# Part of the input projection's weight remainders made ahead, in the first feed-forward, and read back from memory

## The chip, the cores and the metric

One core of a Trainium2 chip runs the whole kernel. The metric is the device time of one execution in microseconds (us), as the median of several runs.

## The reference, cut to what matters

One decoder layer works on 264 tokens (256 of a prompt, 8 of separate samples) of width 2048, all in fp32:

```
h += 1/2 * RMSNorm(SwiGLU_1(RMSNorm(h)))                 2048 -> 2 x 5632 -> 2048
u  = RMSNorm(h);  proj = u @ w_in                        2048 -> 10288 columns: GLU a, b | z | xBC | dt
v  = GLU -> causal depthwise conv (31) -> LayerNorm -> swish
y  = conv (4) on xBC -> SiLU -> chunked state-space scan (48 heads, 8 groups) -> norm gated by SiLU(z)
h += RMSNorm(concat(v, y) @ w_out)                       4096 -> 2048
h += 1/2 * RMSNorm(SwiGLU_2(RMSNorm(h)))
h += RMSNorm(sigmoid(RMSNorm(h) @ W_gate) * (p @ W_proj))
```

Outputs are h and the new convolution and scan states. The change touches only how the weights of `u @ w_in` reach the matrix engine.

## The kernel before, in words

**Three matmuls for one.** Every product with a weight is made in a reduced form of fp32 (`F32R`), with operands split in a high part and a remainder: `x = x_hi + x_lo`, `w = w_hi + w_lo`. `mm3` (L248 to L252) issues `w_hi*x_hi` (L250), `w_hi*x_lo` (L251) and `w_lo*x_hi` (L252) into one accumulator. In the profile `acc` is the accumulator, `act` a split activation (both halves), `whi` and `wlo` the two halves of a weight.

**Weight units.** `PLAN` (L74 to L112) lists all weights in the order of their use as units of at most 16 blocks of 128x128. `Weights.load` (L138 to L157) fetches a unit in two chunks of up to eight blocks (128 partitions x 1024 columns, 512 KB). For each chunk it does three steps: SyncE's queue (SP) issues the DMA `wraw<-in_w` (L153), ScalarE (ACT) rounds it to `whi` (L154), and VectorE (DVE) subtracts `whi` from `wraw` to give `wlo` (L155). Four buffers each of `wraw`, `whi` and `wlo` are two units. `next` (L159) asks for units two ahead of the one in use. A buffer of `whi` or `wlo` comes free when TensorE (PE) has done the last matmul of the chunk four chunks earlier; a buffer of `wraw` comes free when DVE has subtracted the chunk four chunks earlier.

**Stages.** Units 0 to 136 are the first feed-forward (88 gate and up columns, 48 down columns), 137 and 138 the product with `W_proj` (`pproj`), 139 to 219 the 81 units of the input projection, then come the output projection, the second feed-forward and the gate. A unit of 16 blocks is 48 matmuls. `gemm_first` (L340) runs the first units of a matrix with the input index outermost, since its inputs arrive one by one: units 139 to 142 hold four columns (`dt`, B, C, x of group 0) for four of the 16 input blocks each. `gemm_one` (L356) does one column with its 16 input blocks.

**Into the input projection.** L533 to L542 make `u`: for each of 16 blocks k, `tmp = y*rs` (DVE, or GpSimd (POOL) for odd k), `h += tmp` (POOL), two steps later `tmp = h*gain*r` (DVE), a rounding on ACT (L258) and a subtraction on DVE (L259, in the profile L216 `act<-tmp,act`). L545 to L546 then save h in four quarters (`hsave<-h`, on SP's queue).

**Through the input projection.** The loop over `IN_ORDER` (the columns: B, C, three x, three z of each of eight groups, with pairs of GLU columns between) does for each column the convolution or activation on DVE and ACT; after a group's third x column comes `ssd`, whose matmuls, transposes and small DMAs (`ab` L702, `ea` L710, `d_bc` L785, `cbc` L787, `h<-in_hst` L792) run beside the next columns. `finish_gate` closes a group: DVE multiplies y with z (L216 `h<-h,h`, 128x792), ACT squares three parts, POOL adds them (L216 `run<-run,tmp`), PE sums over partitions (L306 `ps<-run,ones`), and ACT and DVE scale. `do_dt` (L571) sends two small arrays through memory (`d_dt`, `d_cs`) before the first `ab` can be loaded.

**Order.** The order of each engine's instructions is set by the framework's scheduler, which places them by a simulated timeline; `load` runs at raised priority. Every engine takes its own list in order, SP's queue of DMAs included: a DMA that waits for a buffer holds all DMAs behind it.

Of the kernel before, what the change touches and what calls it, by code (L numbers as in the profile page):

```python
# [9 lines left out]
F32 = mybir.dt.float32  # L10
F32R = mybir.dt.float32r
AF = mybir.ActivationFunctionType
ALU = mybir.AluOpType
# [6 lines left out]
P = 128  # L20
# [53 lines left out]
def _plan():  # L74

    plan = []
    k16 = list(range(KD))

    def ffn(i):
        gu = f"gu{i}"  # L80
        for q in range(8):
            plan.append((gu, k16[2 * q : 2 * q + 2], list(range(FIRST_FF))))
        for lo, hi in FF_CHUNKS:
            for m in range(max(2 * lo, FIRST_FF), 2 * hi):
                plan.append((gu, k16, [m]))
            for m in range(KD):
                plan.append((f"dn{i}", list(range(lo, hi)), [m]))

    ffn(1)
    for q in range(2):  # L90
        plan.append(("pp", [0, 1], list(range(8 * q, 8 * q + 8))))
    first = [m for _, m in IN_ORDER[:4]]
    for q in range(4):
        plan.append(("in", k16[4 * q : 4 * q + 4], first))
    for _, m in IN_ORDER[4:]:
        plan.append(("in", k16, [m]))
    for q in range(6):
        plan.append(("out", list(range(CM + 4 * q, CM + 4 * q + 4)), [0, 1, 2, 3]))
    for m in range(4, KD, 2):
        for q in range(3):  # L100
            plan.append(("out", list(range(CM + 8 * q, CM + 8 * q + 8)), [m, m + 1]))
    for m in range(0, KD, 2):
        plan.append(("out", list(range(CM)), [m, m + 1]))
    ffn(2)
    for q in range(8):
        plan.append(("pg", k16[2 * q : 2 * q + 2], list(range(FIRST_PG))))
    for m in range(FIRST_PG, KD):
        plan.append(("pg", k16, [m]))
    return plan


PLAN = _plan()  # L112


_COLS = {}
_off = 0
for _n, _w in (
# [10 lines left out]
class Weights:  # L128
# [1 line left out]

    AHEAD = 2

    def __init__(self, tc, pool, w):
        self.tc, self.pool, self.w = tc, pool, w
        self.at = 0
        self.done = []

    def load(self, between=()):  # L138

        tc, nc, i = self.tc, self.tc.nc, len(self.done)  # L140
        n = len(PLAN[i][1]) * len(PLAN[i][2])
        src = self.w[i, :, : n * P].rearrange("p (n c) -> p n c", n=n)
        tiles = []
        with nullcontext() if between else tc.high_priority(offset=1000):
            for a in range(0, n, 8):
                if a // 8 < len(between):
                    between[a // 8]()
                m = min(8, n - a)
                raw, hi, lo = (
                    self.pool.tile([P, 8, P], t, tag=tag, bufs=bufs, name=f"{tag}{i}_{a}")[:, :m, :]  # L150
                    for t, tag, bufs in ((F32, "wraw", 4), (F32R, "whi", 4), (F32R, "wlo", 4))
                )
                self.dma = nc.sync.dma_start(raw, src[:, a : a + m, :])  # L153
                nc.scalar.copy(hi, raw)  # L154
                nc.vector.tensor_tensor(out=lo, in0=raw, in1=hi.bitcast(F32), op=ALU.subtract)  # L155
                tiles += [(hi[:, k, :], lo[:, k, :]) for k in range(m)]
        self.done.append(tiles)  # L157

# [10 lines left out]
def kernel(ctx: ExitStack, tc: tile.TileContext, a: dict):  # L169
    nc = tc.nc  # L170
# [4 lines left out]
    wpool = ctx.enter_context(tc.tile_pool(name="wpool", bufs=4))  # L175
# [4 lines left out]
    dram = ctx.enter_context(tc.tile_pool(name="dram", bufs=1, space=bass.MemoryType.DRAM))  # L180
# [30 lines left out]
    def V(name, i=0):  # L211
        o = _COLS[name][0] + i
        return vec[:, o : o + 1]

    def tt(out, in0, in1, op, eng=None):
        return (eng or nc.vector).tensor_tensor(out=out, in0=in0, in1=in1, op=op)  # L216

    def stt(out, in0, scalar, in1, op0, op1):
        return nc.vector.scalar_tensor_tensor(  # L219
            out=out, in0=in0, scalar=scalar, in1=in1, op0=op0, op1=op1  # L220
        )
# [18 lines left out]
    def act(out, in_, func, bias=0.0, scale=1.0):  # L240
        if func in TABLES:
            table(TABLES[func])
        i = nc.scalar.activation(out=out, in_=in_, func=func, bias=bias, scale=scale)  # L243
        if func in TABLES:
            after(i.ins)
        return i

    def mm3(acc, wt, x, first, last):  # L248
        hi, lo = wt
        nc.tensor.matmul(acc, hi, x[:, 0, :], start=first, stop=False)  # L250
        nc.tensor.matmul(acc, hi, x[:, 1, :], start=False, stop=False)  # L251
        return nc.tensor.matmul(acc, lo, x[:, 0, :], start=False, stop=last).ins  # L252

    def split(x, gain=None):

        t = act_tile()
        if gain is None:
            nc.scalar.copy(t[:, 0, :], x)  # L258
            tt(t[:, 1, :], x, t[:, 0, :].bitcast(F32), ALU.subtract)  # L259
        else:  # L260
            act(t[:, 0, :], x, AF.Identity, scale=gain)
            stt(t[:, 1, :], x, gain, t[:, 0, :].bitcast(F32), ALU.mult, ALU.subtract)
        return t

    class SumSq:
# [3 lines left out]
        def __init__(self, n, tag="run", pool=None, direct=1, fast=False, eng=None, urgent=False):  # L269
            self.n, self.i, self.tag, self.pool = n, 0, tag, pool or apool  # L270
            self.eng, self.urgent = eng or nc.gpsimd, urgent
            self.direct, self.fast, self.parts = direct, fast, []
# [53 lines left out]
    eps1 = cpool.tile([P, 1], F32, name="eps1")  # L326
    nc.gpsimd.memset(eps1, EPS)

    ws = Weights(tc, wpool, a["w"])


    h4 = [h_tile() for _ in range(4)]
# [1 line left out]
    def H(k):  # L334
        return h4[k // 4][:, k % 4, :]
# [18 lines left out]
        return accs  # L354

    def gemm_one(xs, kts, nunits=1):  # L356
        acc = acc_tile()
        n = 0
        for _ in range(nunits):
            for wt in ws.next():  # L360
                mm3(acc, wt, xs[kts[n]], n == 0, n == len(kts) - 1)
                n += 1
        assert n == len(kts)
        return acc

    def ffn(xs, sq, done):
# [27 lines left out]
        def column(m):  # L394
            return accs[m] if m < FIRST_FF else gemm_one(xs, k16)

        ys = [None] * KD
        for c, (lo, hi) in enumerate(FF_CHUNKS):
            for f in range(lo, hi):
                g = gate(column(2 * f))  # L400
                mid(f, g, column(2 * f + 1))
                if bg and f % 2 and f > 2:
                    bg.popleft()()
            for m in range(KD):
                acc = gemm_one(mids, list(range(lo, hi)))
# [50 lines left out]
    ep = ectx.enter_context(tc.tile_pool(name="early", bufs=1))  # L456
# [25 lines left out]

    bg.append(hist_ssm)
    bg.append(hist_mod)


    ysq, hy, yy = (SumSq(KD, f"run{i}", ep, urgent=not i) for i in range(3))
# [32 lines left out]
    for q in range(2):  # L520
        w = ws.next()
# [12 lines left out]
    for k in range(KD + 2):  # L534
        if k < KD:
            t = tmp()
            tt(t, ys[k], rs, ALU.mult, nc.gpsimd if k % 2 and k > 2 else nc.vector)
            tt(H(k), H(k), t, ALU.add, nc.gpsimd if k else nc.vector)
        if k >= 2:
            t = tmp()  # L540
            stt(t, H(k - 2), V("mix_pre", k - 2), r, ALU.mult, ALU.mult)
            us.append(split(t))  # L542
    ectx.close()
    hsave = dram.tile([P, KD, T], F32, name="hsave")
    for q in range(4):  # L545
# [10 lines left out]
        out=tri, in_=tri, pattern=[[1, P]], compare_op=ALU.is_ge, fill=0.0, base=0, channel_multiplier=-1  # L556
# [438 lines left out]
    for k in TAIL_TENSOR:  # L995
        p = tps.tile([P, T], F32, tag="sum", bufs=3, name=nm("sum"))
# [167 lines left out]
```

## Time and profile before

| | |
|---|---|
| median of three runs | 2429.63 us (2427.08 to 2433.99) |
| the profiled execution: its own time, and its span | 2432.44 us, 2430.7 us |
| PE, DVE, ACT, POOL busy, share of the span | 97%, 65%, 49%, 12% |
| DVE's weight subtractions (L155) | 812, 986.9 us in all |
| ACT's weight roundings (L154) | 812, 829.9 us in all |
| moved by DMA, mean rate | 489.89 MB, 202 GB/s |

The span runs from the first to the last instruction of the profiled execution; the 1.7 us between it and the execution's time lie around it. Times in the profile count from the start of the span. The first feed-forward runs to about 772 us, the product with `W_proj` to about 789 us, the input projection to about 1360 us. A row of the windows gives a stretch, its length, the busy time of each engine with its number of instructions, then the clock that TensorE was granted (1.00 is full), the mean busy share of the 16 DMA engines, and GB/s. A row of the waits names who waited for whom, the total in us, how often, and the longest.

### The profile page before, as it was taken

The numbers are of one execution on the slowest core, as the hardware profiler recorded it, in microseconds if no ns is written. First come the engines' busy times: TensorE is split into PE (matmuls) and PEld (weight loads), VectorE is DVE, ScalarE is ACT, GpSimd is POOL, SyncE is SP. The second block draws the span as 40 slices with busy tenths as digits, with TensorE's granted clock in tenths as the row PEclk, the third lists the DMA queues.
The fourth block names the chain that finished last, engine by engine and source line by source line (L and its number), as shares of the span: only waits on it lengthen the run. The fifth ranks groups of instructions, "written<-read, shape, count | busy, mean of one in ns | idle before, by whom it ended". The sixth has DMA issues, their size and how long they took to land.

```text
span 2430.7 us, 47409 instructions
## 1 busy us (share of the span) xinstructions
PE 2367.7 (97%) x19448; PEld 2342.7 (96%) x19448; DVE 1569.2 (65%) x2333; ACT 1181.4 (49%) x1771; POOL 298.4 (12%) x295
## 2 busy tenths in 40 slices
PE   8999999999999889999999999999999999999988
PEld 8999999999999889999999999999999999999988
DVE  6554455545557858988798975766545565565585
ACT  6444444433456465665565545544444443344465
POOL 0400000000015212122122010101000000000103
PEclk9999999999999999999999999999999999999999
DMA  7655555555556666666666556476766776676553
GB/s 249 217 183 184 182 183 182 183 183 183 183 169 207 213 180 193 207 216 202 210 216 205 181 181 216 153 238 228 240 213 223 237 236 217 217 236 206 184 191 132
DMA packets 166250, 489.89 MB, mean 202 GB/s; under 512 B 25568, under 2 KB 42640, under 8 KB 166032
## 3 DMA queue, kind: packets, MB, share of 16 engines
q1 hardware_dynamic: 166032, 486.86, 62.0%
q8 instruction: 152, 2.49, 0.4%
q14 instruction: 66, 0.54, 0.1%
HBM read 465.65 MB, written 22.42 MB: 201 GB/s over the span
## 4 chain that ended last, share of the span: by engine, by line
PE 84%; DVE 6%; issue 3%; ACT 3%; DMA 2%; POOL 1%; SPq 0%; ACTq 0%; POOLq 0%; DVEq 0%
PE acc L250 27%; PE acc L251 27%; PE acc L252 27%; DVE wlo L155 2%; DVE y L219 1%; ACT whi L154 1%; PE ps L306 1%; DVE h L216 1%; DMA ab<-d_cs 1%; DMA cbc<-d_bc 1%; DVE ych L794 1%; PE ps L250 0%; ACT tmp L243 0%; DMA d_bc<-rows 0%; PE ps L251 0%
## 5 line engine op out<-in xcount | busy, mean ns | idle before, releaser
L252 PE MATMUL acc<-act,wlo 128*128 128x264 f32 x6224 | 1770.7, 285 | 4.3 <-DVE wlo L155 4.1
L251 PE MATMUL acc<-act,whi 128*128 128x264 f32 x6224 | 1756.6, 283 | 6.3 <-DVE act L216 6.2
L250 PE MATMUL acc<-act,whi 128*128 128x264 f32 x6224 | 1747.7, 283 | 3.4 <-DVE tmp L216 2.1
L155 DVE TENSOR_TENSOR wlo<-wraw,whi 128x1024 fp32r<-128x1024 f32 (+2 forms) x812 | 986.9, 1217 | 597.9 <-ACT whi L154 595.5
L154 ACT CAST whi<-wraw 128x1024 fp32r<-128x1024 f32 (+2 forms) x812 | 829.9, 1026 | 961.9 <-PE acc L251 717.3
L250 PEld LDWEIGHTS acc<-act,whi 128*128 128x128 f32 x6224 | 1175.5, 190 | 6.0 <-issue 2.1
L251 PEld LDWEIGHTS acc<-act,whi 128*128 128x128 f32 x6224 | 1169.2, 188 | 9.9 <-DVE act L216 7.9
L252 PEld LDWEIGHTS acc<-act,wlo 128*128 128x128 f32 x6224 | 1167.9, 188 | 8.3 <-DVE wlo L155 6.4
L216 POOL TENSOR_TENSOR run<-run,tmp 128x264 f32<-128x264 f32 x93 | 87.8, 944 | 962.9 <-ACT tmp L243 961.8
L216 POOL TENSOR_TENSOR s<-s,eap 128x1024 f32<-128x1024 f32 x24 | 48.8, 2035 | 630.4 <-DMA s<-in_hst 630.4
L219 DVE SCALAR_TENSOR_TENSOR y<-v,vec,y 128x251 f32<-128x251 f32 (+23 forms) x240 | 118.1, 512 | 1.2
L219 DVE SCALAR_TENSOR_TENSOR s<-bb,xds,s 128x128 f32<-128x128 f32 x192 | 52.7, 346 | 66.1 <-POOL s L216 66.1
L216 POOL TENSOR_TENSOR h<-h,cbc 128x512 f32<-128x512 f32 x48 | 73.6, 1553 | 166.0 <-DMA cbc<-d_bc 90.9
L258 ACT CAST act<-tmp 128x264 fp32r<-128x264 f32 x120 | 48.7, 410 | 69.9 <-DVE tmp L216 55.2
L216 DVE TENSOR_TENSOR tmp<-acc,rr 128x264 f32<-128x264 f32 x100 | 43.0, 430 | 51.0 <-PE acc L252 50.8
L216 DVE TENSOR_TENSOR tmp<-tmp,acc 128x264 f32<-128x264 f32 x86 | 36.7, 427 | 38.7 <-PE acc L252 38.6
L216 DVE TENSOR_TENSOR act<-tmp,act 128x264 fp32r<-128x264 f32 x120 | 56.1, 471 | 0.3
L243 ACT ACTIVATE tmp<-tmp 128x264 f32<-128x264 f32 x112 | 47.0, 420 | 8.7 <-DVE tmp L216 8.4
L243 ACT ACTIVATE tmp<-y 128x264 f32<-128x264 f32 x67 | 28.0, 425 | 44.1 <-DVE y L216 43.0
L216 DVE TENSOR_TENSOR y<-y,acc 128x264 f32<-128x264 f32 x80 | 34.0, 425 | 24.0 <-PE acc L252 24.0
L794 DVE TENSOR_REDUCE ych<-h 128x4 f32<-128x512 f32 x48 | 32.4, 678 | 17.5 <-POOL h L216 17.5
L250 PE MATMUL ps<-act,whi 128*128 128x264 f32 x96 | 28.4, 304 | 15.4 <-ACT whi L154 8.1
(165 smaller groups left out, 926.1 us busy)
## 6 DMA issues: line engine op xcount, KB each, us to landing
wraw<-in_w SPq DMA_DIRECT2D x756, 512.0 KB, 4.7
h<-in_hst SPq DMA_DIRECT2D x48, 256.0 KB, 3.9
s<-in_hst SPq DMA_DIRECT2D x24, 512.0 KB, 6.5
out_nss<-s SPq DMA_DIRECT2D x24, 512.0 KB, 3.0
wraw<-in_w SPq DMA_DIRECT2D x24, 384.0 KB, 4.1
wraw<-in_w SPq DMA_DIRECT2D x32, 256.0 KB, 3.9
ab<-d_cs SPq DMA_DIRECT2D x16, 384.0 KB, 5.1
cbc<-d_bc SPq DMA_DIRECT2D x8, 512.0 KB, 4.3
```

What stands on the lines that cost most here:

```text
L154: nc.scalar.copy(hi, raw)
L155: nc.vector.tensor_tensor(out=lo, in0=raw, in1=hi.bitcast(F32), op=ALU.subtract)
L216: return (eng or nc.vector).tensor_tensor(out=out, in0=in0, in1=in1, op=op)
L219: return nc.vector.scalar_tensor_tensor(out=out, in0=in0, scalar=scalar, in1=in1, op0=op0, op1=op1)
L243: i = nc.scalar.activation(out=out, in_=in_, func=func, bias=bias, scale=scale)
L250: nc.tensor.matmul(acc, hi, x[:, 0, :], start=first, stop=False)
L251: nc.tensor.matmul(acc, hi, x[:, 1, :], start=False, stop=False)
L252: return nc.tensor.matmul(acc, lo, x[:, 0, :], start=False, stop=last).ins
L258: nc.scalar.copy(t[:, 0, :], x)
L306: nc.tensor.matmul(p, ones, s, start=i == 0, stop=i == len(self.parts) - 1)
L794: nc.vector.tensor_reduce(out=ych[:, j, b : b + 4], in_=h0, op=ALU.add, axis=AX.X)
```

## The change

`STAGED` lists 30 of the 81 units of the input projection: 139 to 142, then 144, 147, 150 and so on to 219. Their remainders `wlo` are made during the first feed-forward and kept in a new array `low` in the chip's memory (30 x 128 x 2048 fp32).

- **Making them.** `gemm_one` counts its calls; at every odd call it takes one step from a list of 60, which is used up before the first feed-forward ends. A step (`stage`) works on half a unit: a DMA `sraw<-in_w` behind the last weight DMA, a rounding on ACT into `shi` (one buffer), a subtraction on DVE in place in `sraw` (three buffers), and a DMA `low<-sraw`.
- **Using them.** For a staged unit `load` still fetches `wraw` and rounds it to `whi` on ACT. In place of DVE's subtraction SP issues a DMA `wlo<-low` of 512 KB for each chunk. Other units are as before.

The diff, without its empty lines:

```
+def _staged():
+    ins = [i for i, u in enumerate(PLAN) if u[0] == "in"]
+    return ins[:4] + ins[5::3]
+STAGED = _staged()
...
+    def stage(self, pool, s, a):
+        tc, nc = self.tc, self.tc.nc
+        cols = slice(8 * P * a, 8 * P * (a + 1))
+        raw = pool.tile([P, 8 * P], F32, tag="sraw", bufs=3, name=f"sraw{s}_{a}")
+        hi = pool.tile([P, 8 * P], F32R, tag="shi", bufs=1, name=f"shi{s}_{a}")
+        with tc.issue_after(self.dma.ins):
+            nc.sync.dma_start(raw, self.w[STAGED[s], :, cols])
+        nc.scalar.copy(hi, raw)
+        lo = raw.bitcast(F32R)
+        nc.vector.tensor_tensor(out=lo, in0=raw, in1=hi.bitcast(F32), op=ALU.subtract)
+        with tc.issue_after(self.dma.ins):
+            nc.sync.dma_start(self.low[s, :, cols], raw)
...
-                nc.vector.tensor_tensor(out=lo, in0=raw, in1=hi.bitcast(F32), op=ALU.subtract)
+                if i in STAGED:
+                    low = self.low[STAGED.index(i), :, a * P : (a + m) * P]
+                    nc.sync.dma_start(lo.bitcast(F32), low.rearrange("p (n c) -> p n c", n=m))
+                else:
+                    nc.vector.tensor_tensor(out=lo, in0=raw, in1=hi.bitcast(F32), op=ALU.subtract)
...
+    low = dram.tile([len(STAGED), P, 16 * P], F32, name="low")
+    ws = Weights(tc, wpool, a["w"], low)
+    stage, paced = deque(), [0]
...
     def gemm_one(xs, kts, nunits=1):
+        paced[0] += 1
+        if stage and paced[0] % 2:
+            stage.popleft()()
...
+    for i in range(len(STAGED)):
+        for half in range(2):
+            stage.append(lambda i=i, half=half: ws.stage(ep, i, half))
```

Three places show what it moves. A name such as `wlo140_0` is the first chunk of unit 140, `wlo140_8` the second; the last number of a name only tells buffers apart.

First, DVE's list where units 139 to 142 begin, before:

```order
L155 TENSOR_TENSOR wlo140_0_9108<-wraw140_0_9106,whi140_0_9107 128x1024
L219 SCALAR_TENSOR_TENSOR tmp_424_9239<-h_2_86,vec_75,rr_381_9018 128x264
L216 TENSOR_TENSOR act_416_9217<-tmp_415_9215,act_416_9217 128x264
L155 TENSOR_TENSOR wlo140_8_9114<-wraw140_8_9112,whi140_8_9113 128x1024
L216 TENSOR_TENSOR tmp_426_9244<-y_137_2960,rr_376_9000 128x264
L216 TENSOR_TENSOR act_419_9225<-tmp_418_9223,act_419_9225 128x264
L216 TENSOR_TENSOR act_422_9233<-tmp_421_9231,act_422_9233 128x264
L219 SCALAR_TENSOR_TENSOR tmp_427_9247<-h_2_86,vec_75,rr_381_9018 128x264
L155 TENSOR_TENSOR wlo141_0_9346<-wraw141_0_9344,whi141_0_9345 128x1024
```

The same place in DVE's list now:

```order
L246 SCALAR_TENSOR_TENSOR tmp_421_9592<-h_2_87,vec_75,rr_381_9379 128x264
L246 SCALAR_TENSOR_TENSOR tmp_424_9600<-h_2_87,vec_75,rr_381_9379 128x264
L243 TENSOR_TENSOR act_416_9578<-tmp_415_9576,act_416_9578 128x264
L243 TENSOR_TENSOR tmp_426_9605<-y_137_3063,rr_376_9361 128x264
L246 SCALAR_TENSOR_TENSOR tmp_427_9608<-h_2_87,vec_75,rr_381_9379 128x264
L243 TENSOR_TENSOR act_419_9586<-tmp_418_9584,act_419_9586 128x264
L243 TENSOR_TENSOR act_422_9594<-tmp_421_9592,act_422_9594 128x264
L243 TENSOR_TENSOR act_425_9602<-tmp_424_9600,act_425_9602 128x264
```

The eight subtractions of units 139 to 142 are gone from between the steps that make u.

Second, SP's queue of DMAs at the same place, before:

```order
L530 DMA pproj_9021<-act_404_9179 128x528
L153 DMA wraw142_0_9404<-in_w 128x1024
L546 DMA hsave_9319<-h_2_86 128x1056
L153 DMA wraw142_8_9410<-in_w 128x1024
L153 DMA wraw143_0_9464<-in_w 128x1024
L546 DMA hsave_9319<-h_3_87 128x1056
L153 DMA wraw143_8_9470<-in_w 128x1024
L153 DMA wraw144_0_9524<-in_w 128x1024
L546 DMA hsave_9319<-h_4_88 128x1056
```

And SP's queue there now:

```order
L565 DMA pproj_9382<-act_404_9540 128x528
L180 DMA wlo141_0_9707<-low_85 128x1024
L582 DMA hsave_9680<-h_2_87 128x1056
L176 DMA wraw143_0_9825<-in_w 128x1024
L180 DMA wlo141_8_9713<-low_85 128x1024
L176 DMA wraw143_8_9831<-in_w 128x1024
L582 DMA hsave_9680<-h_3_88 128x1056
L180 DMA wlo142_0_9767<-low_85 128x1024
L582 DMA hsave_9680<-h_4_89 128x1056
L180 DMA wlo142_8_9773<-low_85 128x1024
```

The reads of `low` stand in turn with the saves of h and with later weights; each of them waits for PE to free its `wlo` buffer.

Third, SP's queue at the end of group 2's `ssd`, with the small DMAs `d_bc`, `ea` and `cbc`, before:

```order
L153 DMA wraw173_0_12078<-in_w 128x1024
L785 DMA d_bc_9339<-rows_618_11569 8x2x128
L710 DMA ea_652_12073<-d_cs_9338 64x3x128 x2
L787 DMA cbc_619_11572<-d_bc_9339 128x1024
L639 DMA out_xo<-xo_573_11021 128x22
L153 DMA wraw173_8_12084<-in_w 128x1024
```

And there now:

```order
L176 DMA wraw172_0_12318<-in_w 128x1024
L821 DMA d_bc_9700<-rows_618_11930 8x2x128
L746 DMA ea_652_12434<-d_cs_9699 64x3x128 x2
L823 DMA cbc_619_11933<-d_bc_9700 128x1024
L675 DMA out_xo<-xo_573_11382 128x22
L180 DMA wlo171_0_12250<-low_85 128x1024
L176 DMA wraw172_8_12324<-in_w 128x1024
L176 DMA wraw173_0_12439<-in_w 128x1024
L180 DMA wlo171_8_12256<-low_85 128x1024
L176 DMA wraw173_8_12445<-in_w 128x1024
```

Two reads of `low` stand behind `cbc`, which waits for `d_bc` to land.

More of the change, by code (lines that the diff above doesn't have):

```diff
@@ L131, with __init__ @@
     AHEAD = 2
-    def __init__(self, tc, pool, w):
-        self.tc, self.pool, self.w = tc, pool, w
+    def __init__(self, tc, pool, w, low):
+        self.tc, self.pool, self.w, self.low = tc, pool, w, low
         self.at = 0
         self.done = []
+    def stage(self, pool, s, a):
[10 more added lines that the diff above has]
+            nc.sync.dma_start(self.low[s, :, cols], raw)
     def load(self, between=()):
@@ L327 @@
     nc.gpsimd.memset(eps1, EPS)
-    ws = Weights(tc, wpool, a["w"])
+    low = dram.tile([len(STAGED), P, 16 * P], F32, name="low")
+    ws = Weights(tc, wpool, a["w"], low)
+    stage, paced = deque(), [0]
     h4 = [h_tile() for _ in range(4)]
@@ L542 @@
             us.append(split(t))
+    assert not stage
     ectx.close()
```

## The prediction

> **What bounds the kernel now.** I began with the page: its span, the busy times, and the chain that ended last.
>
> ```profile
> span 2430.7 us, 47409 instructions
> PE 2367.7 (97%) x19448; PEld 2342.7 (96%) x19448; DVE 1569.2 (65%) x2333; ACT 1181.4 (49%) x1771; POOL 298.4 (12%) x295
> PE 84%; DVE 6%; issue 3%; ACT 3%; DMA 2%; POOL 1%; SPq 0%; ACTq 0%; POOLq 0%; DVEq 0%
> ```
>
> PE is the bound, and only 63 us of the span is time in which it stands. DVE's 65% is a mean; so I asked next for windows by stage (first feed-forward, the making of u, the first columns, the rest of the input projection).
>
> ```profile
> 46.00:770.00 724.00, 723.55 (x6025) 723.17 (x6024) 386.73 (x437) 317.01 (x411) 61.79 (x102) 1.00 0.58 186
> 785.00:815.00 30.00, 22.85 (x159) 20.96 (x158) 30.00 (x39) 14.78 (x30) 20.21 (x20) 0.94 0.72 247
> 815.00:840.00 25.00, 25.00 (x209) 24.88 (x209) 21.67 (x40) 13.47 (x27) 0.00 (x0) 1.00 0.63 201
> 840.00:1360.00 520.00, 495.17 (x4022) 477.84 (x4021) 423.29 (x726) 301.79 (x555) 99.91 (x75) 0.99 0.65 201
> ```
>
> In the first feed-forward PE never stands and DVE has 47% free. From 785 to 815 DVE is busy all the time and PE loses 7.15 us; from 840 to 1360 DVE is 81% busy and PE loses 24.8 us. The waits of PE say for whom, first in 785 to 815, then in 815 to 1360:
>
> ```profile
> PE acc L251 <- DVE act L216: 6.2, 7, 1.6
> PE acc L250 <- ACT act L258: 0.9, 1, 0.9
> ...
> PE ps L306 <- POOL run L216: 11.8, 8, 2.6
> PE ps L727 <- ACT h L243: 7.3, 2, 4.9
> PE acc L252 <- DVE wlo L155: 4.1, 8, 0.9
> PE ps L753 <- ACT btm L736: 1.1, 1, 1.1
> PE acc L250 <- DVE v L216: 0.4, 1, 0.4
> ```
>
> They sum to 7.1 and 24.7 us, so nearly all of PE's loss is named. Waits cost the clock too: these are two gaps of PE at unit 139, and the windows around them (clock, DMA share, GB/s).
>
> ```profile
> 789.63 0.63 PE L250 MATMUL acc<-act,whi 128*128 128x264 f32 x3 [0.89 <-ACT act L258]
> 791.24 0.59 PE L251 MATMUL acc<-act,whi 128*128 128x264 f32 x1 [0.85 <-DVE act L216]
> ...
> 790.00:792.00 2.00, 0.81 0.91 281
> 792.00:794.00 2.00, 0.50 1.02 404
> 794.00:796.00 2.00, 0.84 0.93 370
> ```
>
> Two gaps under 1 us, close together, halve the clock for about 2 us: 2 us x (0.19 + 0.50 + 0.16) = 1.7 us lost, which is the 0.94 of the 30 us window.
>
> **A, units 139 to 142: about -6 us.** The windows of `wlo` alone (PE, PEld, DVE) give what DVE is freed of:
>
> ```profile
> 785.00:815.00 30.00, 14.13 (x52) 10.44 (x52) 11.20 (x8) 0.94 0.72 247
> 840.00:1360.00 520.00, 344.51 (x1196) 225.98 (x1196) 187.33 (x148) 0.99 0.65 201
> ```
>
> The eight subtractions of 785 to 815 are those of the four staged units: 11.2 of DVE's 30.0 us go. The remaining 18.8 us of DVE and POOL's 20.2 us fit beside what PE needs for four units, 192 matmuls of 0.12 us (723.55 us for 6025), 23 us. So the 7.1 us of waits and the 1.7 us of clock can go, 8.8 us. What is late next is `wlo` itself: eight DMAs now stand in SP's queue among the saves of h. Unit 140's cannot be issued before PE has left unit 138 at 788.7 and is needed by unit 140's third matmuls, 4 x 12 + 8 matmuls = 6.7 us later. Landings are these (the median of the weights, a load that stands behind a weight, the reload of h, the weights at the kernel's start), and the rates at which the DMA engines were full:
>
> ```profile
> wraw<-in_w SPq DMA_DIRECT2D x756, 512.0 KB, 4.7
> s<-in_hst SPq DMA_DIRECT2D x24, 512.0 KB, 6.5
> h<-hsave SPq DMA_DIRECT2D x4, 528.0 KB, 7.4
> ...
> wraw<-in_w SPq DMA_DIRECT2D x10, 512.0 KB, 5.7
> ...
> 9.00:12.00 3.00, 1.00 1.04 405
> 784.00:786.00 2.00, 1.00 0.99 342
> ```
>
> From 785 to 840 the DMA engines moved 30 x 247 + 25 x 201 = 12.4 MB; the reads for the six units staged there (139 to 142, 144, 147; 1.05 MB each) add 6.3. At 405 GB/s, 18.7 MB take 46.2 us of the 55: saving 8.8 us just fits, with no margin. I charge 3 us of new waits for `wlo` and the saves; bounds 0 to 8.8 (as late as DVE was). A is -8.8 + 3, about -6.
>
> By the Trainium skill (TensorE: Matmul & The Clock Gate, Part 1: The HAM clock gate) the clock drops only after an idle window of about 3.4 us; gaps under 1 us would then have cost no clock and A would be -4. The trace disagrees, with 0.50 at 792 to 794.
>
> **B, DVE's queue in the rest of the projection: about -7 us.** 26 staged units take 52 subtractions of 1.27 us (187.33 / 148), 66 us, from the 423 in 840 to 1360: DVE falls from 81% to 69%. Its queue is what PE's largest wait comes from. This is the first gate with such a wait, on DVE, ACT, POOL and PE:
>
> ```profile
> 907.48 1.22 DVE L155 TENSOR_TENSOR wlo<-wraw,whi 128x1024 fp32r<-128x1024 f32 x1
> 910.49 1.22 DVE L155 TENSOR_TENSOR wlo<-wraw,whi 128x1024 fp32r<-128x1024 f32 x1
> 914.75 1.21 DVE L155 TENSOR_TENSOR wlo<-wraw,whi 128x1024 fp32r<-128x1024 f32 x1
> 916.80 1.23 DVE L155 TENSOR_TENSOR wlo<-wraw,whi 128x1024 fp32r<-128x1024 f32 x1
> 918.51 0.98 DVE L216 TENSOR_TENSOR h<-h,h 128x792 f32<-128x792 f32 x1
> 919.52 0.43 ACT L243 ACTIVATE run<-h 128x264 f32<-128x264 f32 x1 [3.70 <-DVE h L216]
> 920.33 3.02 POOL L216 TENSOR_TENSOR run<-run,tmp 128x264 f32<-128x264 f32 x2 [6.23 <-ACT tmp L243]
> 923.41 0.71 PE L306 MATMUL ps<-run,ones 128*128 128x264 f32 x2 [2.57 <-POOL run L216]
> ```
>
> Four subtractions go ahead of the gate's product at 918.51; ACT, POOL and PE wait in turn. A third of them (26 of 77 units) is 1.7 us, against a mean wait of 11.8 / 8 = 1.5 us; but a gate behind unstaged units gains nothing, so I take half of 11.8, 5.9 us. Of the 4.1 us of waits for `wlo`, a third falls on staged units, 1.4 us. Bounds: -16 (both waits gone) and 0 (the list's new order puts the gate as late).
>
> **C, `do_dt`: 0.** The 7.3 us at L727 end a chain through memory; DVE's part shortens and its DMAs meet a fuller queue. Bounds: -7.3 and, three landings each 1.3 us longer (4.7 to about 6), +4.
>
> **D, new waits for `wlo` behind unit 142: +3 us.** A buffer comes free three chunks of 24 matmuls, 8.6 us, before its chunk begins, 8.9 us before its first third matmul. Landing took 4.7 us, 6.5 behind a weight, and 7.4 at worst. Also in SP's way is `cbc`, which waits for `d_bc`; what is queued behind are weights, the loads for the scan, and `wlo`. With 27 MB more in 520 us the DMA share rises from 0.65 to about 0.82 (201 to 253 GB/s), less than the 1.04 at which weights landed in 5.7. So most reads land in time; I charge 3 us for those behind `cbc`. Bounds 0 and the price of the second rival.
>
> **E, the first feed-forward: 0.** 60 steps add 60 x 1.22 us to DVE, 60 x 1.03 to ACT, and 63 MB:
>
> ```profile
> L155 DVE TENSOR_TENSOR wlo<-wraw,whi 128x1024 fp32r<-128x1024 f32 (+2 forms) x812 | 986.9, 1217 | 597.9 <-ACT whi L154 595.5
> L154 ACT CAST whi<-wraw 128x1024 fp32r<-128x1024 f32 (+2 forms) x812 | 829.9, 1026 | 961.9 <-PE acc L251 717.3
> ```
>
> DVE goes to 64% and ACT to 52% of the 724 us, DMA to 273 GB/s at a share near 0.85. The cover: roundings wait for PE (717.3 us), not for data; a chunk has 8.6 us for its 2.3 us of rounding and subtraction, so a step's 2.3 us ahead of it hides. On SP, weights behind a store that waits for DVE are issued four chunks, 11.5 us less 2.3, before PE frees their `whi`, and land in 4.7. If a step were late by more than 4 us, each would cost the rest; I keep +3 as the bound.
>
> **The sum.** -6 - 7 + 0 + 3 + 0 = -10 us. The profiled execution took 2432.44 us, so 2422.4; it stands 2.8 us above the median of 2429.63, and on that the forecast is 2419.6 us. A measurement of this kernel can tell about 0.3%, 7.3 us, from no change.
>
> **Rivals.** *First: DMA is full where u is made.* At the 342 GB/s of 784 to 786, with saves and loads mixed, 18.7 MB take 54.7 of the 55 us: A shrinks to -0.3 and the sum to -4.3, 2425.3 us. For it speaks the share of 0.72 there already; against it, 404 GB/s at 792 to 794. Chance 0.22. By the Trainium skill (DMA: Bandwidth & Descriptors, Where 436 GB/s comes from) transfers between memory and SBUF are held to about 358 GB/s per core: 52.2 us, A -2.8, an estimate of 2422.8 us in all. The trace's 405 GB/s speaks against that as a limit for one core alone.
>
> *Second, slower: `wlo` lands late.* Each of 26 units waits once for what its landing L exceeds 8.9 us. Beyond 9.4 us, 26 x 0.5 = 13 us, A and B are eaten; at 10 us it costs 28.6, so -13 + 28.6, 2445.2 us. For: 7.4 us for the reload of h, reads queued behind `cbc`, and SP held by each `wlo`. Against: 5.7 us in the fullest stretch. Chance 0.17.
>
> *Third: the chain of `do_dt` shortens too.* Two subtractions of unit 144 and two of 147 lie on DVE's way there; C becomes -7.3 and the time 2412.3 us. Chance 0.11.
>
> **The numbers.** My forecast has 0.5: its spread of some 6 us puts 0.40 beyond the 7.3 us and 0.10 within. The first rival gives 0.17 within, 0.03 faster, 0.02 slower; the second 0.16 slower, 0.01 within; the third 0.11 faster. Faster 0.54, same 0.28, slower 0.18. The range reaches down to 2407 (A at its bound, B at -12, C at -2: -22.8) and up to 2437 (D at L of about 9.7 us, 26 x 0.8 = 20.8, A -6, B -7: +7.8). Outside lie most of the second rival beyond, and all gains at once.
>
> **What would show it.** In 46 to 770 PE stays above 723 us, DVE near 460. In 785 to 815 PE's wait for `act` falls below 2 us in total, with at most 4 us on DMAs of `wlo`, landing in 5 to 7.5 us. From 815 to 1360 the wait for `run` halves and DVE's busy time falls by some 66 us. I am wrong if PE's waits for `wlo` exceed 13 us, if the first feed-forward loses more than 3 us, or if the wait for `run` stays near 12 with DVE at 69%: then the order, not DVE's load, made it.

## The result, and the profile after

The changed kernel takes 2457.52 us (median of four, 2447.14 to 2460.99) against 2431.58 us for the kernel before in the same job: ratio 1.0103, 95% interval 1.0075 to 1.0131. The forecast was 2419.6 us, faster; it is 1% slower, and outside the range.

The profiled execution is the fastest of the four, 2447.14 us, 14.7 us over the one of before. What the median adds beyond it, some 10 us, no trace here shows; the three slower executions were granted a mean clock of 0.990 to 0.993, the profiled one 0.994. The page's head, and then the windows that the prediction quoted of before, the last three moved by the 23 us that the input projection now starts later (worked out below):

```profile
span 2445.4 us, 47818 instructions
...
PE 2375.8 (97%) x19448; PEld 2346.9 (96%) x19448; DVE 1548.7 (63%) x2333; ACT 1230.2 (50%) x1831; POOL 290.7 (12%) x295
```

```profile
46.00:770.00 724.00, 713.15 (x5852) 708.62 (x5852) 421.75 (x477) 351.05 (x444) 57.05 (x87) 1.00 0.79 267
...
808.00:838.00 30.00, 23.18 (x171) 21.67 (x171) 25.69 (x40) 16.02 (x34) 17.08 (x20) 0.97 1.02 397
838.00:863.00 25.00, 25.00 (x204) 25.00 (x204) 14.25 (x29) 12.60 (x24) 0.00 (x0) 0.97 0.68 231
863.00:1383.00 520.00, 499.91 (x4076) 483.71 (x4075) 378.85 (x711) 306.20 (x559) 91.31 (x76) 0.99 0.77 255
```

The first row decides: PE did 6025 matmuls in the first feed-forward's 724 us before and does 5852 now, 173 x 0.12 = 20.8 us fewer. While u is made (now 808 to 838, before 785 to 815) the DMA engines are full (1.02 at 397 GB/s, before 0.72 at 247), and PE does hardly more than before: 171 matmuls, before 159.

Both programs have 19448 recorded matmuls, so the start of the n-th can be set against that of the n-th before. The 6400th (782.6 us before, at the end of what precedes u) starts 23.2 us later, the 6800th (842.0 us) 22.2 later, the 10800th (1359.6 us, the end of the projection) 15.9 later, the last 15.0 later. So E cost 23.2 us, A won 1.0, B, C and D together won 6.3. What PE itself waited for in the first feed-forward:

```profile
PE acc L279 <- DVE wlo L182: 5.6, 10, 0.9
PE acc L277 <- ACT act L285: 4.8, 2, 2.4
```

Both come after roundings of ScalarE. These rows show only part of the loss, since a matmul's record is 0.28 us long while starts follow each other every 0.12 us. By the starts, 71 breaks in PE's row cost 19.0 us in 46 to 770 (before 8 breaks, 1.5 us), and a slightly slower pace between them (120.5 ns instead of 120.0) costs 3 us more. On ScalarE and SyncE's queue the waits of the first feed-forward read, parts of two lists:

```profile
ACT shi L155 <- DMA sraw<-in_w: 282.8, 60, 7.5
...
ACT whi L177 <- PE acc L278: 12.8, 13, 1.8
```

```profile
SPq L159 <- DVE sraw L157: 317.1, 55, 8.0
SPq L176 <- DVE wlo L182: 105.3, 107, 3.9
```

A step's rounding waits 282.8 / 60 = 4.7 us for its own load; the weights' roundings, which stand behind it, wait 12.8 us for PE, where they waited 265.2 us in this window before: ScalarE is late, not PE. One period in the timeline (start, length, engine, line, in brackets the idle time before and who ended it):

```profile
298.35 0.43 SPq L154 DMA_DIRECT2D sraw<-in_w  x1
299.10 1.47 SPq L176 DMA_DIRECT2D wraw<-in_w  x2
305.73 1.05 ACT L155 CAST shi<-sraw 128x1024 fp32r<-128x1024 f32 x1 [6.98 <-DMA sraw<-in_w]
306.69 2.00 ACT L177 CAST whi<-wraw 128x1024 fp32r<-128x1024 f32 x2
306.82 1.22 DVE L157 TENSOR_TENSOR sraw<-sraw,shi 128x1024 fp32r<-128x1024 f32 x1 [6.61 <-ACT shi L155]
```

```profile
308.07 0.33 SPq L159 DMA_DIRECT2D low<-sraw  x1
309.21 1.80 SPq L176 DMA_DIRECT2D wraw<-in_w  x2
311.06 0.42 SPq L154 DMA_DIRECT2D sraw<-in_w  x1
312.21 1.80 SPq L176 DMA_DIRECT2D wraw<-in_w  x2
319.58 0.33 SPq L159 DMA_DIRECT2D low<-sraw  x1
```

The load issued at 298.35 ends ScalarE's wait at 305.73, the subtraction ends 308.04, SP's store follows at 308.07, then two weights, then the next step's load at 311.06: a loop through SP, the DMA engines, ScalarE, VectorE and SP again of 311.06 - 298.35 = 12.7 us, for two units that take PE 96 x 0.12 = 11.5 us. From store to store it is 11.5 us this time (319.58 - 308.07). On average over the 60 steps, by the starts of their loads and roundings, a load's rounding follows 6.5 us after its issue and the next step's load 5.3 us after that: a turn of 11.85 us, 0.33 over PE's 11.52, or about 19 us in 59 turns.

In the projection the waits of PE, 790 to 1365 (the same four rows to 1390):

```profile
PE acc L279 <- DMA wlo<-low: 10.3, 11, 1.8
PE ps L763 <- ACT h L270: 5.2, 1, 5.2
PE ps L333 <- POOL run L243: 4.4, 7, 1.4
PE acc L277 <- ACT whi L177: 4.2, 1, 4.2
```

The wait for `run` fell from 11.8 to 4.4, but `wlo<-low` has 10.3 us where VectorE's `wlo` had 4.1, and the rounding of unit 143's first chunk is 4.2 us late: its load, issued at 821.2, landed only at 831.2 in the full engines, and its rounding, at 834.9, stands in ScalarE's list behind those of u's last blocks and of unit 142.

### The profile page after: what moved, and what is told of

It is laid out like the page before. It is cut to its first block, busy times and chain, and to the rows that moved or that the text cites. A ratio compares the mean times of both kernels' runs of the same rounds, so it can differ in the third digit from the quotient of the medians.

```text
span 2445.4 us, 47818 instructions
## 1 busy us (share of the span) xinstructions
PE 2375.8 (97%) x19448; PEld 2346.9 (96%) x19448; DVE 1548.7 (63%) x2333; ACT 1230.2 (50%) x1831; POOL 290.7 (12%) x295
## 4 chain that ended last, share of the span: by engine, by line
PE 54%; DMA 6%; DVE 3%; ACT 1%; issue 1%; POOL 0%; SPq 0%; DVEq 0%; POOLq 0%; ACTq 0%
PE acc L277 17%; PE acc L279 17%; PE acc L278 17%; DMA wlo<-low 2%; DVE wlo L182 1%; DMA d_bc<-rows 1%; DMA cbc<-d_bc 1%; DMA ab<-d_cs 1%; DVE y L246 1%; PE ps L804 1%; PE ps L789 0%; ACT ab L270 0%; DMA h<-in_hst 0%; PE ps L277 0%; DMA s<-in_hst 0%
## 5 line engine op out<-in xcount | busy, mean ns | idle before, releaser
L279 PE MATMUL acc<-act,wlo 128*128 128x264 f32 x6224 | 1771.7, 286 | 16.9 <-DMA wlo<-low 10.3
L182 DVE TENSOR_TENSOR wlo<-wraw,whi 128x1024 fp32r<-128x1024 f32 x752 | 906.6, 1211 | 362.2 <-ACT whi L177 353.7
L177 ACT CAST whi<-wraw 128x1024 fp32r<-128x1024 f32 (+2 forms) x812 | 818.9, 1024 | 574.5 <-PE acc L278 456.0
L157 DVE TENSOR_TENSOR sraw<-sraw,shi 128x1024 fp32r<-128x1024 f32 x60 | 73.8, 1230 | 269.3 <-ACT shi L155 269.3
L155 ACT CAST shi<-sraw 128x1024 fp32r<-128x1024 f32 x60 | 63.0, 1050 | 282.8 <-DMA sraw<-in_w 282.8
L246 DVE SCALAR_TENSOR_TENSOR y<-v,vec,y 128x241 f32<-128x241 f32 (+23 forms) x240 | 114.5, 500 | 2.0
L243 POOL TENSOR_TENSOR h<-h,cbc 128x512 f32<-128x512 f32 x48 | 67.7, 1432 | 171.2 <-DMA cbc<-d_bc 118.9
```

Source lines behind the costliest of these rows:

```text
L246: return nc.vector.scalar_tensor_tensor(out=out, in0=in0, scalar=scalar, in1=in1, op0=op0, op1=op1)
```

## The experiments

The first two kinds of number are measured: the median, and the ratio to the kernel before in the same job. The last three columns come from one trace each, as above: lateness at the 6400th matmul (E), its growth to the 6800th (A), and from there to the 10800th (B, C and D). Kernels whose projection is that of before (make only, traffic only, no store) move by -3.9 to +1.5 in the last column, so less than 4 us is not read there.

| kernel | median us | ratio, 95% interval | E | A | B+C+D |
|---|---|---|---|---|---|
| the change | 2457.52 | 1.0103 (1.0075 to 1.0131) | +23.2 | -1.0 | -6.3 |
| make only | 2448.10 | 1.0079 (1.0059 to 1.0098) | +19.4 | 0.0 | -3.4 |
| no store | 2465.08 | 1.0151 (1.0129 to 1.0174) | +33.2 | 0.0 | -3.9 |
| traffic only | 2432.11 | 1.0009 (0.9999 to 1.0019) | +2.5 | 0.0 | +1.5 |
| use only | 2437.72 | 1.0026 (1.0012 to 1.0040) | +5.9 | -1.0 | -0.2 |
| pipelined | 2433.04 | 1.0009 (1.0000 to 1.0017) | +3.5 | -1.1 | -3.1 |
| no burst | 2428.65 | 0.9998 (0.9988 to 1.0009) | 0.0 | 0.0 | +0.6 |
| burst only | 2435.23 | 1.0026 (1.0018 to 1.0035) | -0.2 | -0.9 | +0.7 |
| reads on ScalarE | 2433.65 | 1.0021 (1.0008 to 1.0033) | +3.4 | -0.7 | -5.6 |
| no low halves | 2410.15 | 0.9921 (0.9908 to 0.9933) | +0.4 | -7.4 | -9.8 |
| reads unused | 2430.96 | 1.0004 (0.9994 to 1.0015) | +0.2 | -2.9 | -0.9 |
| chain on GpSimd | 2447.71 | 1.0074 (1.0062 to 1.0087) | 0.0 | +0.9 | +14.3 |
| before, chain on GpSimd | 2456.54 | 1.0112 (1.0097 to 1.0127) | +0.9 | +0.8 | +20.7 |
| subtractions on GpSimd | 2467.64 | 1.0160 (1.0144 to 1.0175) | +0.5 | 0.0 | +32.1 |

### The steps: make only, no store, traffic only, use only

Make only keeps the steps and lets `load` always subtract:

```
-                if i in STAGED:
+                if False:
```

> The 60 steps of the first feed-forward are made as in the changed kernel, but nothing reads the low halves: all units of the input projection subtract as before. Theory (a step's rounding stands in ScalarE's queue ahead of the weights' and waits for its own load to land, with the subtraction and the store behind it): the whole cost of step E without any gain, 20 to 26 us over before, about 2455 us; ScalarE's waits for sraw stay near 280 us in 46 to 770. Rival (the loss comes where the low halves are read, after 815 us): within 5 us of before. If the steps cost nothing, as forecast: within 3 us of before.

17 us over before by the medians; by the trace 19.4 us are lost at the end of the first feed-forward. ScalarE's wait for `sraw` stays:

```profile
ACT shi L155 <- DMA sraw<-in_w: 246.0, 59, 8.2
```

The steps alone make the loss. No store is make only without the DMA `low<-sraw`:

```
-        with tc.issue_after(self.dma.ins):
-            nc.sync.dma_start(self.low[s, :, cols], raw)
```

> Make only, without the stores: each step still loads, rounds and subtracts in the places that it has in the changed kernel, the low halves go nowhere, and the projection subtracts as before. Theory (the rounding's wait for the landing on ScalarE is what costs, and SyncE's wait for the subtraction adds the rest): at least half of the 17 us of the kernel that makes and stores stay, 8 to 17 us over before, 2440 to 2448 us. Rival (SyncE's wait for the subtraction, with weights behind it, makes all of it): within 4 us of before.

The loss doubles, to 37 us, more than theory or rival had. So the store's wait for the subtraction is not what costs; ScalarE's wait is there in full:

```profile
ACT shi L155 <- DMA sraw<-in_w: 287.5, 60, 8.2
```

The turn of the loop shows why the store is not the point: the next step's load stands behind weights whose buffers come free only after roundings behind the step's own, and so it is issued 5.4 us after the rounding in both kernels, with and without the store. What differs is the time from a load's issue to its rounding, 6.6 us without the store and 6.4 with it: a turn of 12.02 against 11.78 us, and 59 x 0.24 = 14 us, which is the difference in E. Why the loads land later with less traffic, no run tells.

Traffic only loads each half unit and stores it one step later, without rounding or subtraction:

```
+        if n >= 1:
+            ws.stage_store(*parts[n - 1], raws.pop(n - 1))
+        if n < len(parts):
+            raws[n] = ws.stage_load(ep, *parts[n])
```

> In the first feed-forward only the loads of the steps and, one step later, the stores of what was loaded, 63 MB as in the changed kernel; no rounding, no subtraction, and the projection subtracts as before. Theory: nothing waits for a landing in a queue that weights pass, so within 4 us of before, 2428 to 2436 us. Rival 1 (traffic): 15 to 23 us over before, about 2450 us.

As the theory had it: the same bytes, no loss. The window of the first feed-forward:

```profile
46.00:770.00 724.00, 723.54 (x6021) 722.90 (x6020) 385.92 (x434) 314.91 (x408) 61.23 (x101) 1.00 0.82 272
```

Use only makes one slot with two steps and lets every staged unit read it:

```
-                    low = self.low[STAGED.index(i), :, a * P : (a + m) * P]
+                    low = self.low[0, :, a * P : (a + m) * P]
```

> Only two steps are made (one slot of low halves), and all 30 staged units read that one slot from memory: the reads, the missing subtractions and the new order of the projection are all there, the other 58 steps are left out (so the low halves of 29 units are those of the first). Theory (the steps alone cost, the sum A+B+C+D of the forecast is about right): 9 to 11 us under before, about 2421 us; lateness at the end of the first feed-forward under 3 us. Rival (low halves read from memory land late and eat the gain): within 4 us of before or slower.

6.6 us over before, where 10 under was expected. Its two steps alone cost 5.9 us, all of it by the 400th matmul, and by the same wait: the first step's rounding waits 2.1 us for its load on ScalarE, PE then waits 3.0 us for `act`, and from 56.2 to 62 us the granted clock is 0.50. But A and B+C+D, which were to be -10, are -1.2. The theory's second half falls here: the gain isn't there either.

### The steps without the wait: pipelined

The step is split over three calls two units apart, and the rounding is ordered behind the last weight's:

```
+        if n >= 2:
+            ws.stage_store(*parts[n - 2], raws.pop(n - 2))
+        if 1 <= n <= len(parts):
+            ws.stage_make(ep, *parts[n - 1], raws[n - 1])
+        if n < len(parts):
+            raws[n] = ws.stage_load(ep, *parts[n])
...
+        with self.tc.issue_after(self.cast.ins):
+            nc.scalar.copy(hi, raw)
```

> The changed kernel with each step spread over three places, two units apart: the load of part n, the rounding and subtraction of part n-1 (behind the weights' roundings that are already queued) and the store of part n-2. Same work, same bytes. Theory (only the waits for sraw's landing and for the subtraction in the queues cost): step E falls to 0 to 4 us, and the total to 6 to 11 us under before, 2421 to 2426 us; ScalarE's waits for sraw fall from 283 us to under 30. Rival 1 (the traffic of 63 MB more slows the weights): still 15 us lost in the first feed-forward, about 2440 us. Rival 2 (the added 60 roundings and subtractions themselves hold up the weights' chunks): still 10 us or more lost there, about 2435 us or over.

The first feed-forward is whole again with all 60 steps in it (6006 matmuls), and ScalarE waits for PE as before, with no row for `sraw`:

```profile
46.00:770.00 724.00, 723.26 (x6006) 721.44 (x6005) 455.25 (x494) 371.56 (x467) 70.84 (x101) 1.00 0.82 272
```

```profile
ACT whi L187 <- PE acc L288: 250.5, 153, 1.9
```

A rounding and a subtraction per step do hide; what cost was their place in the queues. (Spreading the step and ordering its rounding behind the weight's were not tried apart.) The load now takes 7.5 us to land and the store 8.2, and nobody waits. But the total is only that of before: E's 20 us are won, the forecast's 10 are not there.

### Where the gain went: no burst, burst only, reads on ScalarE

All three are pipelined. No burst doesn't stage the four units that make u, burst only stages just these:

```
-    return ins[:4] + ins[5::3]
+    return ins[5::3]        # no burst
+    return ins[:4]          # burst only
```

> The kernel with pipelined steps, but the four units that make u (139 to 142) subtract as before; 26 units stay staged, 52 steps. Theory (term A came to nothing because the DMA engines are full while u is made, and the low halves and the weights of 143 and 144 land late there; term B is there): DMA share in 785 to 840 as before (0.72 and 0.63) but for unit 144, no wait of 3 us for a rounding near 816, and 2 to 6 us under before, 2425 to 2429 us. Rival (B is given back by waits for the low halves of the 26 units, D): within 2 us of before.

> The kernel with pipelined steps, but only the four units that make u (139 to 142) are staged, 8 steps; the other 26 subtract as before. Theory (the first rival of the prediction, DMA full where u is made): the stretch 785 to 840 wins 0 to 2 us, as the wait for act goes and the waits for wlo and for the rounding of unit 143's or 144's weights come; total within 2 us of before, 2429 to 2433 us. If term A holds without the rest: 5 to 7 us under before, 2425 us.

No burst equals before: its 26 units win nothing. Burst only wins 0.9 us in its stretch and has a median 7 us over before, which its trace (2431.58 us, among its fastest) doesn't show; its executions were granted a mean clock of 0.990 to 0.993, those of before 0.992 to 0.995, so part of it may be clock, and why stays open. In 785 to 815 its DMA engines are full:

```profile
785.00:815.00 30.00, 23.12 (x173) 21.65 (x173) 25.30 (x40) 15.67 (x32) 16.77 (x19) 0.98 1.02 393
```

Reads on ScalarE issues `wlo<-low` from ScalarE, so that it doesn't stand in SyncE's queue:

```
-                    nc.sync.dma_start(lo.bitcast(F32), low.rearrange("p (n c) -> p n c", n=m))
+                    nc.scalar.dma_start(lo.bitcast(F32), low.rearrange("p (n c) -> p n c", n=m))
```

> The kernel with pipelined steps, all 30 units staged, but the reads of the low halves are issued by ScalarE beside the rounding of the same chunk, not by SyncE. Theory 2 (a low half's read stands in SyncE's queue until PE frees its buffer, 24 times for 27 us in 840 to 1360, and holds the weights behind it): PE's waits for wlo fall from 11 us to under 6, and 3 to 6 us less than the pipelined kernel, 2427 to 2430 us. Rival (the DMA engines are the limit, or the landing alone): within 2 us of the pipelined kernel, 2431 to 2435 us.

PE waits only 0.3 us for `wlo<-low`, and waits for `run` instead (pipelined: 11.2 and 6.1):

```profile
PE ps L343 <- POOL run L253: 13.3, 8, 2.4
PE ps L783 <- ACT h L280: 5.6, 1, 5.6
PE acc L287 <- ACT whi L187: 4.7, 1, 4.7
PE acc L289 <- DVE wlo L192: 1.9, 1, 1.9
```

The waits for `wlo` fall as the theory had it, but the time doesn't, so the theory does not hold. `run` and `wlo` together are 15.9 us before, 15.4 after, 17.3 pipelined, 15.5 here. That fits a wait for `wlo` ahead of a gate giving the gate's chain just that much more time; it was not tested by itself.

### Price against gain: no low halves, reads unused

No low halves drops the subtractions of the 30 units and puts nothing in their place:

```
+                if i in STAGED:
+                    lo = hi
```

> The kernel before without the subtractions of the 30 units and without anything in their place: no steps, no reads; the third matmul of these units takes the high half again, so the low halves' share of their products is left out. It is the most that the change could win. Theory 3 (the subtractions were in the way, and the reads' price eats what their absence wins): the wait for act in 785 to 815 goes, the waits for wlo go, 840 to 1360 wins 5 to 8 us, 13 to 17 us under before in all, about 2413 us. Rival (the gate's chain through memory, rows to d_bc to cbc and the loads of h to GpSimd, sets the wait for run whatever VectorE does): 785 to 815 wins 6 to 9 us, 840 to 1360 under 3 us, about 2419 us.

18 us under before: the time that the subtractions cost, in A and in the rest, is real. PE's waits from 785 to 1365:

```profile
PE ps L319 <- POOL run L229: 13.9, 7, 3.4
PE ps L766 <- DVE xde L229: 2.0, 1, 2.0
PE ps L740 <- ACT h L256: 1.9, 1, 1.9
PE acc L264 <- DVE act L229: 1.6, 3, 1.1
PE acc L265 <- DVE wlo L168: 0.3, 1, 0.3
```

Against before, `act` goes from 6.2 to 1.6, `h` of `do_dt` from 7.3 to 1.9 (make only, no store and traffic only, with the projection of before, have 4.9 to 5.4), `wlo` from 4.1 to 0.3. The wait for `run`, on which B rested, is 13.9 against 11.8, with 52 subtractions gone.

Reads unused is the same with the reads back, into the buffers of `wlo`, where no matmul uses them:

```
                 if i in STAGED:
+                    nc.sync.dma_start(lo.bitcast(F32), src[:, a : a + m, :])
                     lo = hi
```

> The kernel without the low halves of the 30 units, but with a read of 512 KB into each buffer of wlo in their place, from SyncE as in the changed kernel; no matmul uses what is read (the third matmul takes the high half again, so the low halves' share is left out), so PE never waits for it. The traffic of the reads is there, the waits for their landing are not. Theory 4 (the bytes cost: weights and the loads of the gate's chain land later): most of the 18 us that the kernel without low halves wins is lost, 0 to 7 us under before, 2421 to 2428 us. Rival (PE's own waits for wlo cost): 12 to 18 us under before, 2411 to 2417 us.

By the medians all 18 us are gone, by the traces 13 of 17, and PE never waits for a read. So the reads cost, and not PE's wait for them. That it is their bytes, and not their place in SyncE's queue, is argued and not shown by this run: SyncE stands some 39 us at these reads for buffers, but in reads on ScalarE they are off its queue and nothing is won. Landings of weights, of the reads and of the scan's loads from 785 to 1360, without the reads and with them:

```profile
wraw<-in_w SPq DMA_DIRECT2D x170, 512.0 KB, 4.8
h<-in_hst SPq DMA_DIRECT2D x45, 256.0 KB, 4.1
```

```profile
wraw<-in_w SPq DMA_DIRECT2D x164, 512.0 KB, 6.2
wlo<-in_w SPq DMA_DIRECT2D x58, 512.0 KB, 6.3
h<-in_hst SPq DMA_DIRECT2D x46, 256.0 KB, 5.6
```

and the stretches, again without and with:

```profile
785.00:815.00 30.00, 28.15 (x222) 26.90 (x221) 27.00 (x41) 18.28 (x37) 17.35 (x20) 1.00 0.80 290
...
840.00:1360.00 520.00, 501.88 (x4103) 487.67 (x4102) 390.01 (x717) 307.71 (x559) 97.86 (x76) 0.99 0.63 206
```

```profile
785.00:815.00 30.00, 25.89 (x202) 24.44 (x201) 25.58 (x40) 16.08 (x34) 17.17 (x20) 1.00 1.02 386
...
840.00:1360.00 520.00, 495.50 (x4029) 480.84 (x4028) 367.76 (x690) 302.94 (x555) 92.82 (x75) 0.98 0.78 254
```

In 785 to 815 full engines (1.02 at 386 GB/s) take 20 matmuls. In 840 to 1360 the share is 0.78, weights and the scan's loads land 1.4 to 1.5 us later, and the gate's wait is the longest of all:

```profile
PE ps L320 <- POOL run L230: 17.6, 8, 3.0
```

### Three ways round, none of use

Chain on GpSimd (no burst, reads on ScalarE) and before, chain on GpSimd, issue the DMAs of the gate's chain from GpSimd:

```
-        nc.sync.dma_start(cbc, d_bc[g, 1].partition_broadcast(P))
+        nc.gpsimd.dma_start(cbc, d_bc[g, 1].partition_broadcast(P))
```

and the same for `d_bc<-rows` and `h<-in_hst`.

> Pipelined steps, 26 units staged (not the four that make u), their reads issued by ScalarE, and the DMAs of the gate's chain (d_bc, cbc and the loads of h for the scan) issued by GpSimd, which uses them, not by SyncE. Theory (with VectorE relieved the gate waits for this chain behind weights in SyncE's queue; off that queue GpSimd's products end earlier): the wait for run falls under 4 us, and 5 to 10 us under before, 2418 to 2423 us. Rival (GpSimd's own issuing and the landings set the chain): within 3 us of before.

> The kernel before with the same three DMAs issued by GpSimd: no unit staged. Theory (in the kernel before VectorE's queue sets the gate, 2.6 to 11.2 us between GpSimd's last product and the gate's): the wait for run stays over 8 us; 0 to 4 us under before, since weights no longer stand behind the waits for d_bc. Rival (the chain set it there too): 5 to 10 us under before.

Both are far slower, where both theories had them faster. PE's wait for `run` was 18.5 us in the first, not under 4, and 14.3 in the second, which stays over 8 as its theory said. GpSimd now waits for these transfers in its own list, with the sums for `run` behind; that this makes the loss was not tested by itself. Subtractions on GpSimd gives it those of the 26 units:

```
+                eng = nc.gpsimd if i in SHARED else nc.vector
+                eng.tensor_tensor(out=lo, in0=raw, in1=hi.bitcast(F32), op=ALU.subtract)
```

> The kernel before, with the subtractions of the 26 units (not the four that make u) on GpSimd instead of VectorE: no steps, no reads. Theory (what is won is VectorE's time, what is lost is traffic; GpSimd is busy 100 of 520 us there and takes some 3 us for 1024 columns by its 1.55 us for 512): up to 6 us under before, 2422 to 2428 us. Rival (GpSimd's queue holds the gate's products, or PE waits for its slow subtraction): 5 to 20 us over before.

37 us over, more than the rival's 5 to 20: one takes 2.5 us, and the scan's products and the gates' sums share GpSimd's list with 121 us of them. PE's waits for `run` (16.3 us) and for these remainders (8.4) are part of the loss; the rest was not followed:

```profile
L157 POOL TENSOR_TENSOR wlo<-wraw,whi 128x1024 fp32r<-128x1024 f32 x48 | 121.2, 2534 | 159.5 <-ACT whi L155 146.4 <-DVE xdt L218 10.1 <-ACT xo L636 3.0
```

No kernel that computes the whole result beats the one before.

## Why the prediction was wrong, point by point

- **E, the failed step: forecast 0 with a bound of +3, measured +23.2.** It said "a chunk has 8.6 us for its 2.3 us of rounding and subtraction, so a step's 2.3 us ahead of it hides". The 2.3 us do hide, as pipelined shows. What it left out is that the rounding stands in ScalarE's list and waits there for its own load, 4.7 us on average and up to 7.5, with the weights' roundings behind it. It priced the step's work and SP's wait for VectorE, but not the wait of ScalarE for the landing, though the weights' landing of 4.7 us was among its rows (the steps' loads land in 6.2). "roundings wait for PE (717.3 us), not for data" held for the weights of before, not for a load that had been issued a few us earlier. And since the next load in turn waits behind weights that wait for these roundings, the delay closes into a loop of 11.85 us, longer than PE's 11.52 for two units.
- **A: forecast -6, measured -1.0.** Its removal was right: without the reads the stretch wins 7.4 of the 8.8 us, and in the changed kernel PE's wait for `act` is 1.4 us. The new price is 7.4 - 1.0 = 6.4 us, not 3. That is the first rival, which gave -0.3: 397 GB/s at a share of 1.02 is the full engine. But the price wasn't the one of either sum. The bytes fitted: from the 6400th to the 6800th matmul 317 GB/s over 58.4 us are 18.5 MB, which 397 GB/s move in 47 us. What was late was one chunk, that of unit 143, whose load took 10 us to land; PE waits 4.2 us for its rounding. With unused reads there is such a wait of 2.2 us, without reads none. The saving fitted "with no margin", by the text's own sum, and should have been rated so. The Trainium skill (DMA: Bandwidth & Descriptors, Where 436 GB/s comes from) holds transfers between memory and SBUF to about 358 GB/s per core, by which the prediction put A at -2.8; its page HBM Reference (Specifications (TRN2)) says that a core streaming alone reaches about 425. The 397 GB/s of this stretch, on one core, lies above the first and below the second, and the engines were full all the same: the share tells it, not the rate.
- **B: forecast -7, the mechanism wrong.** The wait for `run` halves after the change (4.4) and so seems to bear it out, but where no wait for `wlo` stands ahead of the gate it is 13.3 or 13.9 us. That is the text's own mark for a wrong B: "if the wait for `run` stays near 12". Between the 6800th and the 10800th matmul VectorE's busy time fell from 421.4 to 370.2 us, by 51 and not 66, and yet `run` and `wlo` together stayed (15.9 and 15.4 us). So its queue was not the only path to the gates; which other one was as long, no run settles. What falls with VectorE's load is the wait for `wlo` (4.1 to 0.3).
- **C: forecast 0, and it held.** The wait for `h` is 5.2 us, and 4.9 to 5.4 in the three kernels whose projection is that of before. Without reads it falls to 1.9, the third rival's mechanism. With unused reads it is 2.6, so the fuller queue alone does not take that back; what does in the changed kernel stays open.
- **D: forecast +3, measured 10.3 us** of PE waiting for `wlo<-low`, in eleven waits of up to 1.8, one of them (1.2) still where u is made. Its size, not its place, was off; and the run with unused reads shows that this wait isn't even the price: the gain goes as well when PE never waits for a read.
- **Second rival (slower because `wlo` lands late).** The sign came true by another way: landing is 6.8 us in the median, under its 8.9, and E made the loss.

The whole of the projection, -10 in the forecast, is -7.3 in the changed kernel's trace and -1.2 to -6.3 in use only, pipelined and reads on ScalarE, against medians at or above before in each.

## What to carry to other kernels

A background step that loads, computes and stores must be laid over several turns: an engine that takes its list in order waits for the step's own landing, and everything behind it waits too, however little the work is. Cost such a step by its latency at each queue, and by the turn of the loop that these queues close, not by its busy time. And trading an engine's work for a transfer has a price in the stretch even where nobody waits for that transfer: at a DMA share of 0.65, 60 reads of 512 KB cost the 18 us that 60 subtractions had cost.

## What was not expected of the hardware

In the changed kernel PE runs a little slower over long stretches without waiting, at a granted clock of 1.00. The window of 400 to 500 before, and after:

```profile
400.00:500.00 100.00, 100.00 (x836) 100.00 (x835) 52.60 (x59) 40.43 (x49) 0.00 (x0) 1.00 0.58 183
```

```profile
400.00:500.00 100.00, 100.00 (x828) 100.00 (x827) 61.49 (x71) 49.93 (x61) 0.00 (x0) 1.00 0.79 273
```

828 matmuls against 836 is 1%. Traffic only has 836 there at 272 GB/s, so it isn't the traffic; make only has 836 there and 828 in 600 to 700. By the starts it makes some 3 of E's 23 us. In the first feed-forward only the three kernels in which a rounding waits for its step's load all along (the change, make only, no store) have it for long. What sets it wasn't tried.

GpSimd took 2.53 us for the subtraction that takes VectorE 1.22 (the Trainium skill, GPSIMD Engine Reference, 4.1 Engine selection, has it about twice as slow for two inputs, and this agrees), and 0.56 us to issue a DMA of `h<-in_hst` that took SyncE 0.33; its row in the kernel before with the chain on GpSimd:

```profile
L792 POOL DMA_DIRECT2D h<-in_hst x45 | 25.0, 558 | 17.5 <-DVE ych L794 15.9 <-PE acc L251 0.9 <-PE acc L252 0.5
```
